# Low halves of w_out in the last forgetting head: two GpSimd operations instead of one on VectorE

## The chip, the cores and the metric

One core of a Trainium2 chip runs the whole layer. The time is device microseconds (us) of one execution, and the figure compared is the median of several executions. Engines are named as in the profile: PE (TensorE, matmuls), PEld (its weight loads), DVE (VectorE), ACT (ScalarE), POOL (GpSimd), SP (SyncE, which here only issues DMAs).

## The reference, cut to what matters

One decoder layer, 2048 tokens, width 1024. Two mixers share one normalised and modulated input and one input projection: 8 heads of forgetting attention (causal softmax with a cumulative log-gate bias) and 8 heads of sliding-window attention. Both are gated, put side by side and sent through w_out (1024 x 1024).

```python
oa = forgetting_attention(qa, ka, va, fa + b_fgate[l])
oa = oa * jax.nn.silu(za)
...
ob = ob * jax.nn.silu(zb)
y = jnp.concatenate([oa, ob], axis=-1) @ w_out[l]
x = x + gate[:, None, :] * rms_norm(y, g_post[l])
```

## The kernel before, in words

All large products are done in float16 with each operand split into a high and a low half, so that high x high, high x low and low x high add up to nearly float32. A split is always the same pair of steps: ScalarE writes the high half (a scaled copy, rounded to float16), then another engine subtracts it from the scaled value and writes the rest as the low half.

The order of the work is written out by hand. Each engine runs its instructions in program order; an instruction that waits holds up those behind it on its engine. The forgetting heads run as 160 steps, 20 for each head (`Step`). In the loop over the steps, `s` is the step, `hd` the head and `r` the step within the head. A step does in turn:

- ScalarE exponentials of the scores (`exp32`, L1263), 128 x up to 1024 float32 into a tile called p;
- the subtraction of the step before on VectorE (`low`, L1270), p minus its high half, both in SBUF; this is the operation called pha in the profile;
- in the last head (`hd == 7`) the split of one or two tiles of w_out (`w_out_split`, L1345 and L1346);
- half of the step's fillers, the high half of p on ScalarE (L1267), the score matmuls of the next step (L1256 to L1259, the tile sta), the value matmuls of two steps before (L1280 to L1283), and the rest of the fillers.

Fillers are, until the middle of the last head, matmuls for row maxima of the scores (L1207), which VectorE reduces from PSUM (L1210, L1212); from step 10 of the last head on they are units of the output product (`Out.product`, L1405, three matmuls each: high x high, oz high x w low, oz low x w high). Before its product an output block is turned: PE transposes it (L1368), VectorE multiplies by the gate path (L1377, in place in T), ScalarE squares it (L1381, tile zj), VectorE and ScalarE split it (tile oz, L1391 and L1392).

w_out is cut into 16 tiles m of 128 x 512 float32 (m modulo 8 is the row block k, m // 8 the column half). A table gives the step of the last head in which each is split:

```python
w_at = {2: [0], 3: [1], 4: [2], 5: [3], 6: [4], 8: [5], 10: [6], 11: [7], 12: [8], 13: [9], 14: [10],
        15: [11, 12], 16: [13, 14], 17: [15]}
```

Loads (L1340, on SP) are issued three steps ahead into a ring of 6 buffers (`stp`), which also takes the junk outputs zj (L1381) and yj (L1414) of ScalarE. A buffer is given out again when all its readers are done. Both halves go into one resident tile, wohl; the product reads row block k of the first column half from unit 0 on (step 10) and of the second half from unit 16 on (step 15). So tiles 11 to 15, split in steps 15 to 17, are read by PE in steps 16 and 17.

GpSimd runs the product of the rotary embedding (L711, early in the program), small copies, and issues DMAs. Its last instruction before the end is the DMA of a z tile at 969.20 us, ahead of the first split.

Of the kernel before, what the change touches and what calls it, by code (L numbers as in the profile page):

```python
# [15 lines left out]
ALU = mybir.AluOpType  # L16
# [24 lines left out]
def hybrid_layer(  # L41
# [17 lines left out]
    V, A, G, PE, SP = nc.vector, nc.scalar, nc.gpsimd, nc.tensor, nc.sync  # L59
# [97 lines left out]
    wsc = const.tile([P, KT], F32, name="wsc")  # L157
# [1156 lines left out]
    def w_slot(n):  # L1314
        return oio["w"][:, n // KT, n % KT, :]
# [26 lines left out]
    def w_out_split(m):  # L1342
        k, cc = m % KT, slice((m // KT) * CH, (m // KT + 1) * CH)
        raw, hi = w_raw.pop(m), w_slot(k)[:, cc]
        A.activation(hi, raw[:], AF.Copy, scale=wsc[:, k:k + 1])  # L1345
        V.scalar_tensor_tensor(w_slot(8 + k)[:, cc], raw[:], wsc[:, k:k + 1], hi, op0=ALU.mult, op1=ALU.subtract)  # L1346

    oio = {}

# [117 lines left out]
    with tc.manual_schedule():  # L1467
# [27 lines left out]
        for s, stp_ in enumerate(steps):  # L1495
# [28 lines left out]
            if hd == 7:  # L1524
                for m in w_at.get(r, []):
                    w_out_split(m)
# [70 lines left out]
```

## Time and profile before

| | |
|---|---|
| time, median of 3 executions | 1220.45 us (1219.6 to 1221.59) |
| span of the profiled execution | 1218.0 us |
| its own time | not recorded beside the span |
| PE busy | 1164.0 us, 96% |
| VectorE busy | 907.5 us, 75% |
| ScalarE busy | 675.5 us, 55% |
| GpSimd busy | 142.1 us, 12% |
| the 16 w_out subtractions on VectorE (L1346) | 984.8 to 1037.2 us, 745 ns median |
| the 16 high halves on ScalarE (L1345) | 982.3 to 1036.4 us, 709 ns median |

Busy time says how long an engine had work; a busy share is an average over stages with different limits, so the change has to be read in its own stretch. Rows of the timeline read: start, duration, engine, line, operation, output <- inputs, and in brackets how long the engine sat idle before it and what ended that. Rows of one line's instructions give minimum/median/maximum in ns, then the first and last start. Rows of the windows give the stretch, its length, and the busy us (with the count) of PE, PEld, DVE, ACT and POOL, then the granted PE clock (1.00 is full), the DMA share and GB/s.

### The profile page before, as it was taken

What the parts mean: (1) busy time and instruction counts of PE and PEld (TensorE: products, weight loads), DVE (VectorE), ACT (ScalarE), POOL (GpSimd) and SP (SyncE); (2) the same over time, 40 slices, a digit from 0 to 9 for tenths busy, and PEclk for the clock granted to TensorE, in tenths of its full rate; (3) what the DMA queues carried; (4) which work ended last, traced back from release to release, by engine and by line L of the source; (5) the groups of instructions that cost most, each with busy time, mean ns of one, the idle gap of its engine ahead of it and who ended that gap; (6) DMA issues with size and microseconds to landing.
All of it is one profiled execution on the core that took longest, in us unless ns stands there. A gap on an engine that the chain in (4) does not pass through costs nothing.

```text
span 1218.0 us, 27395 instructions
## 1 busy us (share of the span) xinstructions
PE 1164.0 (96%) x10832; PEld 695.9 (57%) x10832; DVE 907.5 (75%) x2268; ACT 675.5 (55%) x1117; POOL 142.1 (12%) x252
## 2 busy tenths in 40 slices
PE   6789999999999999999999999999999979999996
PEld 2457545865558976555555555555555545555553
DVE  6766557676776747688888798878978797666665
ACT  2666445555655452566667666666766778333231
POOL 2011133223232211011010110010000000000000
PEclk9899999999999999999999999999999989999999
DMA  9554332323323322323334323122111135445652
GB/s 325 187 146 139 81 89 79 86 56 103 93 69 86 57 58 52 76 59 84 83 60 84 86 61 79 39 71 49 38 46 42 58 118 186 144 156 190 202 167 81
DMA packets 88036, 120.71 MB, mean 99 GB/s; under 512 B 27836, under 2 KB 63716, under 8 KB 87908
## 3 DMA queue, kind: packets, MB, share of 16 engines
q1 hardware_dynamic: 76932, 85.94, 23.5%
q0 software_dynamic: 10976, 33.03, 11.6%
q8 instruction: 85, 1.39, 0.6%
q14 instruction: 43, 0.35, 0.1%
HBM read 71.56 MB, written 25.18 MB: 79 GB/s over the span
## 4 chain that ended last, share of the span: by engine, by line
PE 77%; DVE 9%; DMA 5%; issue 3%; ACT 2%; SPq 2%; POOL 1%; DVEq 0%; ACTq 0%; POOLq 0%
PE bk L307 29%; PE bk L1405 12%; PE bk L325 7%; PE sta L1256 4%; PE bk L1207 4%; PE sta L1257 4%; PE poa L1282 2%; PE poa L1283 2%; PE poa L1280 2%; PE pxb L864 2%; PE pss L831 2%; PE pob L883 2%; DVE pha L1270 1%; DVE a_m L1210 1%; PE bk L1368 1%
## 5 line engine op out<-in xcount | busy, mean ns | idle before, releaser
L1263 ACT ACTIVATE p<-sta,lift,scl_qk 128x1024 f32<-128x1024 f32 (+2 forms) x160 | 172.0, 1075 | 135.3 <-PE sta L1257 76.8
L307 PE MATMUL bk<-hT,wh_qk 128*128 128x512 f16 x768 | 194.6, 378 | 0.4 <-DVE a_m L1210 0.4
L1405 PE MATMUL bk<-wohl,oz 128*128 128x512 f16 x768 | 172.4, 379 | 1.7 <-ACT wohl L1345 0.8
L1210 DVE TENSOR_REDUCE a_m<-bk 128x1 f32<-128x512 f32 x192 | 130.2, 685 | 52.4 <-PE bk L1207 51.7
L1270 DVE TENSOR_TENSOR pha<-p,pha 128x1024 f16<-128x1024 f32 (+2 forms) x160 | 169.0, 1056 | 0.0
L1267 ACT ACTIVATE pha<-p 128x1024 f16<-128x1024 f32 (+2 forms) x160 | 148.0, 925 | 5.9 <-PE poa L1283 0.9
L1405 PEld LDWEIGHTS <-oz 128*128 128x128 f16 x768 | 74.4, 99 | 83.7 <-issue 1.8
L1280 PE MATMUL poa<-vt,pha 128*128 128x65 f16 x1088 | 117.4, 193 | 2.7 <-DVE ona L1289 2.7
L1283 PE MATMUL poa<-vt,pha 128*128 128x65 f16 x1088 | 117.2, 193 | 1.1 <-DVE pha L1270 1.1
L1282 PE MATMUL poa<-vt,pha 128*128 128x64 f16 x1088 | 117.5, 195 | 0.0
L1256 PE MATMUL sta<-T 128*128 128x512 f16 (+1 forms) x320 | 112.2, 351 | 4.7 <-ACT p L1263 4.6
L307 PEld LDWEIGHTS <-wh_qk 128*128 128x128 f16 x768 | 72.4, 97 | 75.2 <-issue 1.4
L1280 PEld LDWEIGHTS <-pha 128*128 128x128 f16 x1088 | 102.4, 97 | 17.4 <-DVE ona L1289 3.8
L1207 PE MATMUL bk<-T 66*128 66x512 f16 (+2 forms) x320 | 109.9, 350 | 2.0 <-DMA T<-stq 1.5
L1257 PE MATMUL sta<-T 69*128 69x512 f16 (+1 forms) x320 | 111.1, 352 | 0.0
L1282 PEld LDWEIGHTS <-pha 128*128 128x128 f16 x1088 | 101.5, 97 | 11.5 <-issue 0.3
L1283 PEld LDWEIGHTS <-pha 128*128 128x128 f16 x1088 | 101.5, 99 | 1.3 <-DVE pha L1270 1.3
L307 PE MATMUL bk<-hT,wh_za 128*128 128x512 f16 x384 | 99.8, 378 | 0.0
L325 PE MATMUL bk<-wh_va,hT 128*128 128x128 f16 x1536 | 91.0, 219 | 0.6 <-issue 0.6
L307 PE MATMUL bk<-hT,wh_zb 128*128 128x512 f16 x384 | 89.9, 379 | 1.1 <-DVE wh_zb L251 1.1
L325 PEld LDWEIGHTS <-hT 128*128 128x128 f16 x1536 | 87.4, 98 | 5.7 <-issue 3.1
L307 PE MATMUL bk<-hT,wh_qb 128*128 128x512 f16 x384 | 87.2, 379 | 0.0
(491 smaller groups left out, 1886.1 us busy)
## 6 DMA issues: line engine op xcount, KB each, us to landing
wa<-in_w_ada_dram SPq DMA_DIRECT2D x16, 512.0 KB
z_d<-tz POOLq DMA_DIRECT2D x32, 256.0 KB, 3.5
T<-stq SPq DMA_DIRECT2D x128, 64.0 KB
T<-o_d SPq DMA_DIRECT2D x16, 512.0 KB
T<-z_d SPq DMA_DIRECT2D x16, 512.0 KB
xr<-in_x_dram SPq DMA_DIRECT2D x16, 512.0 KB
out_dram<-yg SPq DMA_DIRECT2D x15, 512.0 KB
xt<-in_x_dram SPq DMA_DIRECT2D x12, 512.0 KB
```

The source lines that it names most:

```text
L307: PE.matmul(ps, whl[:, a, k, :], hT[ci][:, b, k, :], start=(k == 0 and n == 0), stop=(k == KT - 1 and n == 2))
L325: PE.matmul(ps[:, u * P:(u + 1) * P], hT[ci][:, a, k, u * P:(u + 1) * P], whl[:, b, k, :], start=(k == 0 and n == 0), stop=(k == KT - 1 an ...
L1207: PE.matmul(mx[:, :w], T[0:XM, 0, i * P:(i + 1) * P], T[0:XM, 2, pc * CH:pc * CH + w], start=True, stop=True)
L1256: PE.matmul(self.st[:, o:o + w], T[:, 3, kb_], T[:, 1, qc], start=True, stop=False)
L1257: PE.matmul(self.st[:, o:o + w], T[0:XR, 2, kb_], T[0:XR, 0, qc], start=False, stop=not diag)
L1263: A.activation(self.p32[:, :self.w], self.st[:, :self.w], AF.Exp, scale=scl[f"qk{self.hd}"][:], bias=lift[:])
L1267: A.activation(self.ph[:, 0, :self.w], self.p32[:, :self.w], AF.Copy)
L1270: V.tensor_tensor(self.ph[:, 1, :self.w], self.p32[:, :self.w], self.ph[:, 0, :self.w], op=ALU.subtract)
L1280: PE.matmul(po[:, u, :], ph[:, 0, pq], vt[:, b, hd, 0:65], start=(self.first and n == 0 and u == 0), stop=False)
L1282: PE.matmul(po[:, u, 0:64], ph[:, 0, pq], vt[:, b, hd, 65:VW], start=False, stop=False)
L1283: PE.matmul(po[:, u, :], ph[:, 1, pq], vt[:, b, hd, 0:65], start=False, stop=(self.last and n == len(self.blocks) - 1))
L1405: PE.matmul(py, self.hl[:, i, k, :], w_slot(8 * j + k)[:, cc], start=(k == 0 and m_ == 0), stop=(k == KT - 1 and m_ == 2))
```

## The change

`w_out_split` no longer subtracts on VectorE. GpSimd first scales the raw tile in place, then subtracts the high half from it:

```diff
         A.activation(hi, raw[:], AF.Copy, scale=wsc[:, k:k + 1])
-        V.scalar_tensor_tensor(w_slot(8 + k)[:, cc], raw[:], wsc[:, k:k + 1], hi, op0=ALU.mult, op1=ALU.subtract)
+        G.tensor_scalar(raw[:], raw[:], wsc[:, k:k + 1], None, op0=ALU.mult)
+        G.tensor_tensor(w_slot(8 + k)[:, cc], raw[:], hi, op=ALU.subtract)
```

Since the scaling writes the tile that ScalarE reads, it has to wait for ScalarE's high half; the subtraction waits for the scaling. Lines below L1346 move down by one (L1377 becomes L1378, L1405 becomes L1406).

On VectorE, at the first two tiles (steps 2 and 3 of the last head), the subtractions go and nothing else moves. The wo names are raw tiles of w_out, wohl the resident halves, pha and p the halves and the exponentials of a step, bk PSUM banks:

```order
 L1210 TENSOR_REDUCE a_m<-bk_134 128x1
 L1270 TENSOR_TENSOR pha<-p_14278,pha 128x384
-L1346 SCALAR_TENSOR_TENSOR wohl<-wo_14272,wsc,wohl 128x512
 L1212 ISA bk_135,a_m<-bk_135,cmask 128x128
 L1212 ISA a_m 128x1
```

Each stood right behind a pha subtraction, and the reductions behind it move up by one place.

On GpSimd, behind its last DMAs and at the end of the program, there now stand 32 instructions, two for each tile; these are the first of them, after the z tiles:

```order
 L349 DMA z_d<-tz 128x512 x6
-L1593 UNCONDITIONAL_BRANCH
-L1593 ISA
+L1346 TENSOR_SCALAR wo_14272<-wo_14272,wsc 128x512
+L1347 TENSOR_TENSOR wohl<-wo_14272,wohl 128x512
+L1346 TENSOR_SCALAR wo_14274<-wo_14274,wsc 128x512
+L1347 TENSOR_TENSOR wohl<-wo_14274,wohl 128x512
```

and these the last, tiles 11 to 15, which PE reads at once:

```order
+L1346 TENSOR_SCALAR wo_14776<-wo_14776,wsc 128x512
+L1347 TENSOR_TENSOR wohl<-wo_14776,wohl 128x512
+L1346 TENSOR_SCALAR wo_14778<-wo_14778,wsc 128x512
+L1347 TENSOR_TENSOR wohl<-wo_14778,wohl 128x512
+L1346 TENSOR_SCALAR wo_14830<-wo_14830,wsc 128x512
+L1347 TENSOR_TENSOR wohl<-wo_14830,wohl 128x512
+L1346 TENSOR_SCALAR wo_14832<-wo_14832,wsc 128x512
+L1347 TENSOR_TENSOR wohl<-wo_14832,wohl 128x512
+L1346 TENSOR_SCALAR wo_14873<-wo_14873,wsc 128x512
+L1347 TENSOR_TENSOR wohl<-wo_14873,wohl 128x512
```

All tiles now pass through one engine in turn, two operations each, with no other work of that engine between them. Loads, junk outputs and product units that waited for VectorE's subtraction of a tile wait for GpSimd's; the order of PE, ScalarE and SP is the same.

## The prediction

> **What bounds the kernel now.** I read the busy shares first, then the 2 and 10 us windows around the last forgetting head, then single instructions there in order of time.
>
> ```profile
> span 1218.0 us, 27395 instructions
> PE 1164.0 (96%) x10832; PEld 695.9 (57%) x10832; DVE 907.5 (75%) x2268; ACT 675.5 (55%) x1117; POOL 142.1 (12%) x252
> 980.00:990.00 10.00, 6.49 (x70) 3.54 (x70) 9.83 (x23) 9.12 (x12) 0.00 (x0) 1.00 0.22 67
> 990.00:1000.00 10.00, 9.21 (x105) 6.00 (x106) 10.00 (x18) 6.26 (x8) 0.00 (x0) 0.83 0.74 236
> 1020.00:1030.00 10.00, 10.00 (x83) 5.15 (x81) 5.53 (x8) 8.15 (x12) 0.00 (x0) 1.00 0.59 191
> 1030.00:1040.00 10.00, 8.79 (x106) 5.52 (x103) 7.90 (x11) 8.94 (x13) 0.00 (x0) 1.00 0.01 2
> ```
>
> Over the span PE is the bound (96%). The change touches only the stretch from 982 to 1038 us. In the window rows (length, then busy us of PE, PEld, DVE, ACT and POOL, then the granted PE clock) it has three parts: until 1000 VectorE has no idle time (9.83 and 10.00 of 10 us) and PE waits (6.49); at 1020 to 1030 PE is full and VectorE half idle (5.53); at 1030 to 1040 PE waits again. GpSimd is empty throughout.
>
> **What is removed.** Sixteen VectorE operations:
>
> ```profile
> L1346 DVE SCALAR_TENSOR_TENSOR wohl<-wo,wsc,wohl x16: 743/745/752, 984.8 to 1037.2; 128x512 f16<-128x512 f32 x16
> 986.84 1.21 DVE L1270 TENSOR_TENSOR pha<-p,pha 128x1024 f16<-128x1024 f32 x1
> 987.97 0.74 DVE L1346 SCALAR_TENSOR_TENSOR wohl<-wo,wsc,wohl 128x512 f16<-128x512 f32 x1
> 988.63 0.68 DVE L1210 TENSOR_REDUCE a_m<-bk 128x1 f32<-128x512 f32 x1
> ```
>
> Durations overlap a little; from start to start one costs 988.63 - 987.97 = 0.66 us, and a 1024-wide pha subtraction 1.13. Five (m = 0 to 4) stand in the stretch where VectorE is the bound: 5 x 0.66 = **3.3 us** off the path. The other eleven lie where VectorE has idle time or the product waits for them.
>
> **What is added.** Each tile gets two GpSimd operations in place of one on VectorE. The subtraction has a direct neighbour, the same shape with two inputs; the scaling has none:
>
> ```profile
> L711 POOL TENSOR_TENSOR qs<-qs,sinT x20: 1256/1269/1356, 63.7 to 385.2; 128x512 f32<-128x512 f32 x20
> L499 POOL TENSOR_SCALAR_AFFINE_SELECT bm<-zero 128x256 f32<-128x256 f32 x1 | 0.4, 414 | 0.0
> L842 POOL COPY sm__1821<-snk 128x2 f32<-128x2 f32 x2 | 0.3, 194 | 0.0
> ```
>
> Subtraction: 1.27 us. Scaling, unknown: the one-input rows give (414 - 194) / 254 = 0.87 ns per element, so 194 + 510 x 0.87, about 0.65 us; its ends are 0.41 (half the width) and 1.27 (the two-input operation). I take 0.65, the one-input slope, and 0.04 for each of two handovers (a guess): a pair is **2.0 us**. The Trainium skill (GPSIMD Engine Reference, section 3.1) gives 769 ns for a 512-element loop; with that a pair would be 2.1 and the sum 1.2 us higher; no row here shows it.
>
> **Who blocks whom.** Does work on GpSimd leave VectorE alone? Rows where the rotary product (L711) overlapped VectorE:
>
> ```profile
> 63.70 1.27 POOL L711 TENSOR_TENSOR qs<-qs,sinT 128x512 f32<-128x512 f32 x1 [55.63 <-DMA qs<-qf]
> 64.71 1.47 DVE L251 SCALAR_TENSOR_TENSOR wh_zb<-wr_zb,w_sw,wh_zb 128x512 f16<-128x512 f32 x2 [0.41 <-ACT wh_zb L245]
> L251 DVE SCALAR_TENSOR_TENSOR wh_zb<-wr_zb,w_sw,wh_zb x8: 740/745/808, 64.7 to 312.4; 128x512 f16<-128x512 f32 x8
> L384 DVE TENSOR_SCALAR xt<-xt,rst x8: 748/748/1755, 85.3 to 112.5; 128x1024 f32<-128x1024 f32 x8
> L848 DVE TENSOR_SCALAR b_nb<-b_m x32: 169/170/694, 161.1 to 425.4; 128x4 f32<-128x4 f32 x32
> ```
>
> It does not. A VectorE scaling went from 0.75 to 1.76 us, a tiny one from 0.17 to 0.69. The kind that matters, two inputs in SBUF, met GpSimd once, in the last 0.26 us of its operation, and took 808 instead of 745 ns: 0.06 lost of 0.26 possible. The pha subtraction (L1270) has two SBUF inputs, one for each step of the head. I take a wait to the end of the GpSimd operation; the ends are none and a full 1.27 for each. The skill (SBUF — State Buffer, Who interferes with whom) says of this kind that it contends with a GpSimd instruction that reads SBUF and that the loser blocks fully; by it the sum is my forecast, by 0.06 us a wait the first stretch would gain 3.0 instead. The 63 ns agree in sign only.
>
> **First stretch, worked out.** GpSimd may start on a tile when ScalarE's high half is done (L1345):
>
> ```profile
> 982.28 0.72 ACT L1345 ACTIVATE wohl<-wo,wsc 128x512 f16<-128x512 f32 x1
> 984.94 0.71 ACT L1345 ACTIVATE wohl<-wo,wsc 128x512 f16<-128x512 f32 x1
> 987.48 0.71 ACT L1345 ACTIVATE wohl<-wo,wsc 128x512 f16<-128x512 f32 x1
> 982.15 1.08 DVE L1270 TENSOR_TENSOR pha<-p,pha 128x896 f16<-128x896 f32 x1
> 984.30 0.55 DVE L1270 TENSOR_TENSOR pha<-p,pha 128x384 f16<-128x384 f32 x1
> 990.12 1.22 DVE L1270 TENSOR_TENSOR pha<-p,pha 128x1024 f16<-128x1024 f32 x1
> 993.12 1.08 DVE L1270 TENSOR_TENSOR pha<-p,pha 128x896 f16<-128x896 f32 x1
> 995.86 0.55 DVE L1270 TENSOR_TENSOR pha<-p,pha 128x384 f16<-128x384 f32 x1
> 998.19 1.27 DVE L1377 TENSOR_TENSOR T<-bk,T 128x512 f32<-128x512 f32 x2
> ```
>
> Tile 0: scaling after the pha operation in progress, 983.20 to 983.85; subtraction to 985.17. VectorE's next pha, ready at 984.30, waits 0.87. Tile 1: scaling 985.70, subtraction 986.40 to 987.67; the pha of 986.84, now 0.21 late, waits 0.62. Tile 2: after that pha, subtraction to 990.82; the next waits 0.53. Likewise 0.82 and 0.92 for the pha operations of 993.12 and 995.86, since GpSimd is behind by then and busy without a break. Waits of 0.87 + 0.62 + 0.53 + 0.82 + 0.92 = 3.76 against 3.30 saved: **+0.5 us** at L1377 (998.19), on which ScalarE's squares and the next scores hang. Ends: -3.3 (no wait) and 5 x 1.27 - 3.3 = +3.1.
>
> **Middle (m = 5 to 10): 0.** What hides a late low half is PE's own work (10.00 of 10 us) and one to eight steps between split and use (closest: tiles 7 and 10, one step). Behind waiting instructions stand: on SP the later w_out loads, which wait for a buffer that GpSimd now frees, and behind them an o_d store and the loads of x; on ScalarE the junk outputs (zj, yj), which take the same buffers, and behind them the next exponentials. None comes due before a pair has finished; if the cover is gone, each costs up to one pair, 2.0.
>
> **Last tiles.** Tiles 11 to 15 come in a burst, and PE uses them at once:
>
> ```profile
> 1028.39 1.32 ACT L1345 ACTIVATE wohl<-wo,wsc 128x512 f16<-128x512 f32 x2
> 1031.65 1.32 ACT L1345 ACTIVATE wohl<-wo,wsc 128x512 f16<-128x512 f32 x2
> 1029.13 1.21 DVE L1270 TENSOR_TENSOR pha<-p,pha 128x1024 f16<-128x1024 f32 x1
> 1031.59 1.22 DVE L1270 TENSOR_TENSOR pha<-p,pha 128x1024 f16<-128x1024 f32 x1
> 1035.25 1.22 DVE L1270 TENSOR_TENSOR pha<-p,pha 128x1024 f16<-128x1024 f32 x1
> 1037.16 0.75 DVE L1346 SCALAR_TENSOR_TENSOR wohl<-wo,wsc,wohl 128x512 f16<-128x512 f32 x1 [0.70 <-ACT wohl L1345]
> 1034.28 2.10 PE L1405 MATMUL bk<-wohl,oz 128*128 128x512 f16 x9
> 1037.97 0.59 PE L1405 MATMUL bk<-wohl,oz 128*128 128x512 f16 x2 [0.41 <-DVE wohl L1346]
> ```
>
> Today the last low half is ready at 1037.91 and PE, which waited 0.41 for it, goes on. GpSimd can begin tile 11 at 1029.1 and needs five pairs, 10.0 us, plus the three pha subtractions that take turns with it, 3 x 1.13 = 3.4: ready at 1042.5, so **+4.6 us**. PE has nothing else then: L1405 stands in front of the next scores. After 1040 the end of the program is a PE chain, so the delay is passed on whole. Ends: without turns 1029.1 + 10.0 = 1039.1, +1.2; with the scaling at 1.27 (pairs of 2.6) and four turns, 1029.1 + 13.1 + 4.5 = 1046.7, +8.8.
>
> **Sum.** +0.5 + 0 + 4.6 = +5.1 us: the span goes from 1218.0 to 1223.1. The profiled execution's own time is not among the records; its span is 2.45 below the median of 1220.45, so the time is 1220.45 + 5.1 = **1225.5 us**.
>
> **Rivals.**
>
> *VectorE wins the turns.* If a waiting VectorE operation, or one issued in the same moment, always goes first, the first stretch keeps its 3.3 and only the tail pays: -3.3 + 4.6 = +1.3, 1221.8. For it: all three long cases above can also be read as GpSimd merely having started first. Against: in all five cases worked out above GpSimd is already in its subtraction when the pha operation becomes ready.
>
> *The clock falls in the tail.* After two stretches of PE waiting the granted clock (last but two) halved:
>
> ```profile
> 988.00:990.00 2.00, 0.32 (x8) 0.15 (x6) 1.97 (x6) 2.00 (x4) 0.00 (x0) 1.00 0.00 0
> 992.00:994.00 2.00, 2.00 (x27) 1.52 (x26) 2.00 (x4) 1.12 (x2) 0.00 (x0) 0.50 0.46 135
> 1000.00:1002.00 2.00, 0.21 (x1) 0.10 (x1) 1.97 (x5) 2.00 (x4) 0.00 (x0) 0.88 0.67 203
> 1002.00:1004.00 2.00, 2.00 (x12) 1.18 (x11) 1.86 (x7) 1.60 (x3) 0.00 (x0) 0.50 0.01 4
> 1000.00:1010.00 10.00, 8.12 (x71) 5.66 (x70) 8.41 (x18) 8.69 (x12) 0.00 (x0) 0.66 0.52 165
> ```
>
> From 1034 to 1042 PE would run three groups of 0.65 us and wait otherwise, as thin as 988 to 990. The first fall took 10 x (1 - 0.83) = 1.7 us of PE's work, the second 10 x (1 - 0.66) = 3.4: 1227.2, up to 1228.9.
>
> *Faster: GpSimd does not hold VectorE.* The first stretch gives 3.3, and with the squares 3.3 earlier PE's idle time before 1001.8 goes, so that the half clock after 1002 (at least 1.7 of PE's work) is not granted; the tail costs its lower end, 1.2: -3.3 - 1.7 + 1.2 = -3.8, 1216.6; with the clock as it is -2.1, 1218.3. It decides where the five waits together stay below 3.3 - 1.2 = 2.1 us, 0.42 each. For it: the one overlapping two-input operation lost 63 ns. Against: it met only the end of a GpSimd operation.
>
> *Slow scaling.* With 1.27 for it: +3.1 at most and +8.8, 1232.
>
> **How the numbers follow.** Forecast 0.42; clock 0.22; VectorE wins 0.14; not held 0.15 (half of it with the clock gained); slow scaling 0.07. The range reaches from 1217.5 (part of the not-held case) to 1231: left out are 0.07 below, and 0.07 with a part of the clock case above. About 0.2% (2.4 us) is what a measurement tells from no change, so faster means below 1218.0 and slower above 1222.9. Faster 0.13 (not held, most of it, and the spread of the others), same 0.20 (VectorE wins, the rest of not held, the forecast's low edge), slower 0.67.
>
> **What would show it.** Scaling near 0.65 and subtraction near 1.27 us on GpSimd; pha subtractions (L1270) between 982 and 998 of 1.8 to 2.1 us instead of 1.2; L1378 (L1377 before) of the first block within 1 us of 998.2; PE waiting 4 to 5 us for GpSimd's L1347 between 1032 and 1043; and the granted clock after 1040. Unchanged pha durations would make the prediction wrong in its first term and most of its last; a tail wait under 2 us, in its size.

## The result and the profile after

The changed kernel takes 1229.24 us (median of 4, 1228.83 to 1230.65) against 1220.87 (median of 4, 1219.6 to 1221.59): ratio 1.0067, 95% interval 1.0051 to 1.0082, which is +8.2 us (6.2 to 10.0). Slower, as forecast, and inside the range, but 8.2 where the sum said 5.1. The profiled execution took 1230.65 with a span of 1228.9, the longest of the four.

The two added operations and the engine that waits for them, in the rows of one line (minimum/median/maximum ns, first and last start) and of PE's waits (us in total, times, longest):

```profile
L1346 POOL TENSOR_SCALAR wo<-wo,wsc x16: 1559/1569/2917, 986.1 to 1043.5; 128x512 f32<-128x512 f32 x16
L1347 POOL TENSOR_TENSOR wohl<-wo,wohl x16: 1150/1157/1551, 987.8 to 1045.2; 128x512 f16<-128x512 f32 x16
PE bk L1406 <- POOL wohl L1347: 7.7, 6, 2.0
```

The scaling takes 1.57 us, not the 0.65 of the sum, and is longer than the two-input subtraction behind it (1.16). Unhindered, a pair is 2.78 us from start to start (1040.74 to 1043.52 below). The first stretch, VectorE and then GpSimd:

```profile
985.20 1.08 DVE L1270 TENSOR_TENSOR pha<-p,pha 128x896 f16<-128x896 f32 x1
989.22 1.49 DVE L1270 TENSOR_TENSOR pha<-p,pha 128x1024 f16<-128x1024 f32 x1
992.12 1.38 DVE L1270 TENSOR_TENSOR pha<-p,pha 128x1024 f16<-128x1024 f32 x1
994.61 1.53 DVE L1270 TENSOR_TENSOR pha<-p,pha 128x896 f16<-128x896 f32 x1
997.14 0.60 DVE L1270 TENSOR_TENSOR pha<-p,pha 128x384 f16<-128x384 f32 x1
999.29 1.29 DVE L1378 TENSOR_TENSOR T<-bk,T 128x512 f32<-128x512 f32 x2 [0.36 <-DMA T<-z_d]
```

```profile
988.95 1.56 POOL L1346 TENSOR_SCALAR wo<-wo,wsc 128x512 f32<-128x512 f32 x1
991.72 1.57 POOL L1346 TENSOR_SCALAR wo<-wo,wsc 128x512 f32<-128x512 f32 x1
994.51 1.57 POOL L1346 TENSOR_SCALAR wo<-wo,wsc 128x512 f32<-128x512 f32 x1
```

To compare these rows with those of before: the pha row of 985.20 stands ahead of the first split and was at 982.15, so this execution was 3.05 us late before any changed instruction. Other executions below are 0.2 to 5.6 late at that row, with the same program up to it. All positions are therefore counted from this row (the **anchor**). The T row (L1378) then comes 14.09 behind it, against 998.19 - 982.15 = 16.04: the first stretch **gained** 1.95 us, where I had a loss of 0.5. The last four of the five pha operations lost 0.28 + 0.16 + 0.45 + 0.05 = 0.94 against their rows of before, not 3.76, and the first (987.35, not shown) lost nothing. With the 3.30 saved and the 0.36 us that the T row waited for its load of z_d, this accounts for the stretch: 3.30 - 0.94 - 0.36 = 2.00.

In the middle, one wait that was not in the sum:

```profile
1014.33 1.87 DVE L1393 SCALAR_TENSOR_TENSOR oz<-T,w_pw,oz 128x1024 f16<-128x1024 f32 x1 [0.22 <-ACT oz L1392]
1015.11 2.92 POOL L1346 TENSOR_SCALAR wo<-wo,wsc 128x512 f32<-128x512 f32 x1
1019.32 0.59 PE L1406 MATMUL bk<-wohl,oz 128*128 128x512 f16 x2 [0.78 <-POOL wohl L1347]
```

Here GpSimd is the one that is held up: its scaling of tile 7 reaches 2.92 us beside VectorE's split of oz and the pha operation behind that (0.55 us at 1016.13, not shown), the pair ends late, and PE stands 0.78 us. In the tail, GpSimd's rows and PE's:

```profile
1030.98 2.58 POOL L1346 TENSOR_SCALAR wo<-wo,wsc 128x512 f32<-128x512 f32 x1 [1.43 <-ACT wohl L1345]
1036.43 1.55 POOL L1347 TENSOR_TENSOR wohl<-wo,wohl 128x512 f16<-128x512 f32 x1
1040.74 1.56 POOL L1346 TENSOR_SCALAR wo<-wo,wsc 128x512 f32<-128x512 f32 x1
1043.52 1.56 POOL L1346 TENSOR_SCALAR wo<-wo,wsc 128x512 f32<-128x512 f32 x1
1045.17 1.15 POOL L1347 TENSOR_TENSOR wohl<-wo,wohl 128x512 f16<-128x512 f32 x1
```

```profile
1034.86 0.59 PE L1406 MATMUL bk<-wohl,oz 128*128 128x512 f16 x2 [0.86 <-POOL wohl L1347]
1038.03 0.81 PE L1406 MATMUL bk<-wohl,oz 128*128 128x512 f16 x3 [0.77 <-POOL wohl L1347]
1040.81 0.81 PE L1406 MATMUL bk<-wohl,oz 128*128 128x512 f16 x3 [1.97 <-POOL wohl L1347]
1043.59 1.44 PE L1406 MATMUL bk<-wohl,oz 128*128 128x512 f16 x3 [1.97 <-POOL wohl L1347]
1046.37 1.01 PE L1406 MATMUL bk<-wohl,oz 128*128 128x512 f16 x2 [1.34 <-POOL wohl L1347]
```

PE waits 6.91 us in the tail. GpSimd runs five pairs without a gap from 1030.98 to 1045.17 + 1.15 = 1046.32. Three such matmuls take 0.81 us at 1040.81 and 1.44 at 1043.59: the clock has fallen between. By windows of 2 us the granted clock is 1.00 at 1038 to 1040, 0.98 at 1040 to 1042 and 0.50 at 1042 to 1044. The windows of 10 us show the same, first before, then after the change (PE busy first, granted clock third from the end):

```profile
1040.00:1050.00 10.00, 8.90 (x118) 5.68 (x115) 7.46 (x24) 4.45 (x7) 0.00 (x0) 1.00 0.00 1
```

```profile
1040.00:1050.00 10.00, 5.87 (x35) 2.85 (x35) 0.69 (x1) 1.71 (x4) 6.15 (x5) 0.60 0.01 2
```

From the last low half to the end of the span it is 1228.9 - 1046.32 = 182.58 us, against 1218.0 - 1037.91 = 180.09: another 2.5. So, in positions from the anchor: -1.95 to the T row, +0.69 to the pha operation of 1030.92 (1029.13 before), +6.62 to the last low half, +2.49 behind it: 7.85 in all.

### The profile page after: what moved, and what is told of

The parts are those of the page before. It is cut to its first block, busy times and chain, and to the rows that moved or that the text cites. A ratio compares the mean times of both kernels' runs of the same rounds, so it can differ in the third digit from the quotient of the medians.

```text
span 1228.9 us, 27422 instructions
## 1 busy us (share of the span) xinstructions
PE 1167.3 (95%) x10832; PEld 696.9 (57%) x10832; DVE 900.8 (73%) x2252; ACT 675.2 (55%) x1117; POOL 190.2 (15%) x284
## 5 line engine op out<-in xcount | busy, mean ns | idle before, releaser
L1406 PE MATMUL bk<-wohl,oz 128*128 128x512 f16 x768 | 175.0, 382 | 8.8 <-POOL wohl L1347 7.7
L1406 PEld LDWEIGHTS <-oz 128*128 128x128 f16 x768 | 74.7, 100 | 92.2 <-issue 10.7
```

The source lines that it names most:

```text
L1406: PE.matmul(py, self.hl[:, i, k, :], w_slot(8 * j + k)[:, cc], start=(k == 0 and m_ == 0), stop=(k == KT - 1 and m_ == 2))
```

## The experiments

The theory after the result: **the burst**. Tiles 11 to 15 pass through GpSimd at 2.8 us each while PE reads them at once; the waits and the half clock make up the loss, and the early tiles are a small gain. Rivals: GpSimd costs VectorE time wherever they meet (**holding**); the late start of the profiled execution belongs to the changed program (**offset**). Each ratio is to the kernel before, with its 95% interval.

### Tiles 11 to 15 back on VectorE, and the mirror image

```diff
+        if m < 11:
             G.tensor_scalar(raw[:], raw[:], wsc[:, k:k + 1], None, op0=ALU.mult)
             G.tensor_tensor(w_slot(8 + k)[:, cc], raw[:], hi, op=ALU.subtract)
+        else:
+            V.scalar_tensor_tensor(w_slot(8 + k)[:, cc], raw[:], wsc[:, k:k + 1], hi, op0=ALU.mult, op1=ALU.subtract)
```

> Tiles 0 to 10 split by GpSimd as in the changed kernel, tiles 11 to 15 by VectorE as before. Theory A (burst): the whole loss comes from tiles 11 to 15, whose GpSimd pairs of 2.8 us PE waits for, and the half clock after them; the first stretch gained about 2 us. Then the PE waits for L1347 go from 7.7 to under 0.5 us, the granted clock at 1040 to 1050 is 1.00 again, and the time is 1220.9 - 2.0 = 1218.9 (1217.5 to 1220). Theory B (holding): GpSimd takes time from VectorE wherever the two meet, in the middle tiles too; then eleven of sixteen tiles keep their share and the time stays at 1222 or above. Theory C (offset): the 3.05 us that the profile of the changed kernel was late before its first changed instruction belongs to the changed program; then 1222 at the least.

The mirror image has `if m >= 11` in place of `if m < 11`.

> The mirror image: tiles 0 to 10 on VectorE as before, tiles 11 to 15 on GpSimd. Theory A: the tail loses its 7.3 us of waiting and 2.5 us behind the last subtraction, and no gain of the first stretch stands against it: 1220.9 + 9.8 = 1230.7, about 2 us slower than the changed kernel (1229.5 to 1232). Theory B: only five of sixteen tiles pay, and the time is about 1220.9 + 8.4 x 5/16 = 1223.5. PE waits for L1347 near 8 us by A, near 3 by B.

Measured: 0.9992 (0.9981 to 1.0003) with the tail on VectorE, 1.0086 (1.0069 to 1.0103) with only the tail on GpSimd, +10.5 us (8.4 to 12.6). This speaks for the burst and against the offset: five tiles cost no less than all sixteen (1.0067), and the profile of the first kernel is only 0.85 us late at its anchor. The mirror image:

```profile
983.88 1.08 DVE L1270 TENSOR_TENSOR pha<-p,pha 128x896 f16<-128x896 f32 x1
1045.11 1.15 POOL L1348 TENSOR_TENSOR wohl<-wo,wohl 128x512 f16<-128x512 f32 x1
```

Ahead of its tail all stands as before the change (the T row 16.04 behind the anchor, the pha operation at the tail's start 46.99), and the last low half comes 62.38 behind it, against 55.76. So the tail alone costs 6.6 us, what it cost in the changed kernel, and the rest of the program 1.95 more (1228.3 - 1046.26 = 182.04), 8.6 in all by the trace. PE's waits for GpSimd are 6.1 us, not the 8 expected.

The first kernel kept half of what was expected:

```profile
983.00 1.08 DVE L1270 TENSOR_TENSOR pha<-p,pha 128x896 f16<-128x896 f32 x1
997.07 1.29 DVE L1381 TENSOR_TENSOR T<-bk,T 128x512 f32<-128x512 f32 x2
1017.42 0.59 PE L1409 MATMUL bk<-wohl,oz 128*128 128x512 f16 x2 [0.77 <-POOL wohl L1348]
1029.01 1.22 DVE L1270 TENSOR_TENSOR pha<-p,pha 128x1024 f16<-128x1024 f32 x1
```

It leads by 1.97 us at the T row (14.07 behind the anchor, against 16.04) and by 0.97 at the last row (46.01, against 46.98); between them stands the wait for tile 7, so my "under 0.5 us" of PE waits for GpSimd failed.

### Only tiles 0 to 4 on GpSimd

```diff
-        if m < 11:
+        if m < 5:
```

> Only tiles 0 to 4 on GpSimd, tiles 5 to 15 on VectorE as before. The kernel with tiles 0 to 10 on GpSimd was 1.97 us ahead at the first T row and 0.97 ahead at 1029; between them PE waited 0.77 us for tile 7's GpSimd subtraction. Theory M (that wait is what was given back): without it the first stretch's gain stays, 1220.9 - 1.9 = 1219.0, ratio 0.998, no PE wait for GpSimd, and the pha operation at about 1029 comes 1.5 to 2 us earlier than before, after allowing for the stretch ahead of the first split. Rival (the gain is lost in any case, to the next wait for ScalarE or to the half clock): 1220 to 1221.

Measured: 0.9983 (0.9971 to 0.9995).

```profile
1032.22 1.22 DVE L1270 TENSOR_TENSOR pha<-p,pha 128x1024 f16<-128x1024 f32 x1
```

In its trace PE waits for GpSimd nowhere, and this pha operation leads by 2.55 us (1032.22 - 987.79 = 44.43, against 46.98), where 1.5 to 2 were expected. The lead at the T row (1.92) is kept, as theory M has it; by the times alone this kernel and the one with eleven tiles are not told apart, since their intervals overlap.

### All tiles on GpSimd, one a step

```diff
-        w_at = {2: [0], 3: [1], 4: [2], 5: [3], 6: [4], 8: [5], 10: [6], 11: [7], 12: [8], 13: [9], 14: [10],
-                15: [11, 12], 16: [13, 14], 17: [15]}
+        w_at = {2: [0], 3: [1], 4: [2], 5: [3], 6: [4], 7: [5], 8: [6], 9: [7], 10: [8], 11: [9], 12: [10],
+                13: [11], 14: [12], 15: [13, 14], 16: [15]}
```

> All tiles on GpSimd as in the changed kernel, but split about one a step from step 7 on (5 in step 7, 6 in 8, 7 in 9, 8 in 10, 9 in 11, 10 in 12, 11 in 13, 12 in 14, 13 and 14 in 15, 15 in 16), so that no tile is read within a pair's time. Theory A (burst): GpSimd has the throughput (a pair of 2.8 to 4.2 us against steps of 3 to 4), PE waits for its subtractions fall from 8.5 us to under 1, the clock at 1040 to 1050 is 1.00, and the time is 1219 to 1221. Rival (what GpSimd takes from VectorE costs anyway, wherever it stands): 1224 or above.

Measured: 1.0008 (0.9997 to 1.0019), so 7.2 us of the 8.2 are gone with every GpSimd operation still there. The granted clock at 1040 to 1050 is 1.00. The holding rival (1224 or above) falls: on the scale of 1220.87 this is 1221.9 (1220.5 to 1223.2). It is also a little above the 1219 to 1221 that theory A gave.

```profile
1038.08 0.59 PE L1406 MATMUL bk<-wohl,oz 128*128 128x512 f16 x2 [1.97 <-POOL wohl L1347]
```

This is PE's one wait for GpSimd, for tile 15, still the third pair of a small burst, and not the "under 1" that I expected.

### Is it the scale, the form, or the operation?

```diff
-        G.tensor_scalar(raw[:], raw[:], wsc[:, k:k + 1], None, op0=ALU.mult)
+        G.tensor_tensor(raw[:], raw[:], wsc[:, k:k + 1].broadcast_to([P, CH]), op=ALU.mult)
```

> The changed kernel with the scaling written as a two-input product with the scale broadcast along the row. Expected 1.16 us for it, as for the subtraction, instead of 1.57: a pair of 2.37 instead of 2.78, so 5 x 0.41 = 2.0 us less in the tail (PE waits 5.7 instead of 7.7). Theory H (each kind holds VectorE's two-input operations for a part of its own: the trace reads as 0.56 us of the scaling's 1.57 and 1.02 of the subtraction's 1.16): the two-input scaling holds VectorE 0.46 us longer, the pha subtractions of the first stretch lose 2 to 4 us together instead of 0.94, and the time is 1227 to 1229. Rival (the part held is the same whatever the form): they lose about 0.9 still, and the time is 1226 to 1227.

```diff
-        G.tensor_scalar(raw[:], raw[:], wsc[:, k:k + 1], None, op0=ALU.mult)
+        G.tensor_scalar(raw[:], raw[:], 1.0, None, op0=ALU.mult)
```

> The changed kernel with the scaling by the constant 1.0 in place of the per-partition scale (so the low halves are not those of the scaled weights). If the scale read from a tile is what makes the scaling 1.57 us instead of the 0.65 of my sum, it falls to 0.6 to 0.8, a pair to about 1.9, and the tail by 5 x 0.9 = 4.5 us and the clock: 1222 to 1225. If the operation itself has that price, 1.57 stays and the time is that of the changed kernel, 1228 to 1230.

Measured: 1.0069 (1.0045 to 1.0092) and 1.0064 (1.0044 to 1.0083). The scaling's rows, of the broadcast product and of the constant:

```profile
L1346 POOL TENSOR_TENSOR wo<-wo,wsc x16: 1030/1040/2066, 987.3 to 1046.0; 128x512 f32<-128x512 f32 x16
```

```profile
L1346 POOL TENSOR_SCALAR wo<-wo x16: 1479/1491/2517, 985.0 to 1042.0; 128x512 f32<-128x512 f32 x16
```

The scale read from a tile is worth 0.08 us; the scalar operation itself is the dear one, and the two-input product is cheaper by half a microsecond. Yet the kernel with the cheaper scaling is no faster: on the scale of 1220.87 it takes 1229.3, and theory H had 1227 to 1229. Its first stretch loses what theory H said, for the most part through another cause:

```profile
986.32 1.08 DVE L1270 TENSOR_TENSOR pha<-p,pha 128x896 f16<-128x896 f32 x1
988.47 1.48 DVE L1270 TENSOR_TENSOR pha<-p,pha 128x384 f16<-128x384 f32 x1
991.29 1.96 DVE L1270 TENSOR_TENSOR pha<-p,pha 128x1024 f16<-128x1024 f32 x1
994.65 1.81 DVE L1270 TENSOR_TENSOR pha<-p,pha 128x1024 f16<-128x1024 f32 x1
997.59 1.96 DVE L1270 TENSOR_TENSOR pha<-p,pha 128x896 f16<-128x896 f32 x1
1000.54 0.97 DVE L1270 TENSOR_TENSOR pha<-p,pha 128x384 f16<-128x384 f32 x1
1002.62 1.27 DVE L1378 TENSOR_TENSOR T<-bk,T 128x512 f32<-128x512 f32 x2
```

```profile
988.39 1.15 POOL L1347 TENSOR_TENSOR wohl<-wo,wohl 128x512 f16<-128x512 f32 x1
994.22 1.16 POOL L1347 TENSOR_TENSOR wohl<-wo,wohl 128x512 f16<-128x512 f32 x1
1000.05 1.04 POOL L1346 TENSOR_TENSOR wo<-wo,wsc 128x512 f32<-128x512 f32 x1 [1.46 <-ACT wohl L1345]
```

The first pha operation behind a subtraction, 0.08 us after its start, takes 1.48 instead of 0.55: held until 988.47 + 0.93 = 989.40, 1.01 us into the subtraction's 1.15. In the changed kernel the pha operations behind a scaling were held until 0.55, 0.56 and 0.55 us into its 1.57 (989.50 - 988.95, 992.28 - 991.72, 995.06 - 994.51). With two-input operations only, the five pha operations lost 0.93 + 0.75 + 0.59 + 0.88 + 0.42 = 3.57 us, and the T row is 0.26 later than before (1002.62 - 986.32 = 16.30).

Only the last of the five stands behind the product (1000.05), which held it for 0.91 of its 1.04. The four before it stand behind the subtraction, which is the same in the changed kernel; it held them until 1.01 to 1.03 us into it. So the product does hold longer than the scalar form, as theory H has it, but most of the loss comes from where the pha operations fall: with the shorter pair they become ready during the subtraction. The kernel with a half scaling below keeps the scalar form, and its pha operations lose 2.96 us, all but 0.12 of it behind the subtraction. What the cheaper scaling gave back in the tail (+5.2 us there against +6.6) the first stretch took.

### The clock: PE kept busy while it waits

```diff
+            if (self.t, n) == (0, 1):
+                for _ in range((0, 0, 0, 3, 3, 8, 8, 5)[k]):
+                    PE.matmul(py, self.hl[:, 0, k - 1, :], w_slot(k - 1)[:, cc], start=False, stop=False)
             for m_, (i, j) in enumerate(((0, 0), (0, 1), (1, 0))):
```

> The changed kernel with 27 matmuls more in front of the five units that wait for tiles 11 to 15 (3, 3, 8, 8, 5), repeating a high product of the unit before, so that PE works while it waits; their sums are added to that block, so the output differs. Theory K (the half clock at 1040 to 1050 comes from PE standing idle): the granted clock there goes from 0.60 to 0.95 or more, the end of the program comes 2.5 us sooner after the last subtraction (180.1 us as before the change, not 182.6), and the time is 1226 to 1227. Rival (the clock follows something else, or its loss is hidden): the clock stays below 0.8 and the time is 1228.5 to 1231, the added matmuls costing up to 1 us.

Measured: 1.0037 (1.0024 to 1.0049), 3.7 us less than the changed kernel with 27 matmuls more.

```profile
1040.00:1050.00 10.00, 8.62 (x64) 4.32 (x62) 1.38 (x4) 2.94 (x6) 6.06 (x5) 1.00 0.01 2
1041.15 1.89 PE L1407 MATMUL bk<-wohl,oz 128*128 128x512 f16 x8
1043.50 0.59 PE L1409 MATMUL bk<-wohl,oz 128*128 128x512 f16 x2 [0.24 <-POOL wohl L1347]
1045.07 1.15 POOL L1347 TENSOR_TENSOR wohl<-wo,wohl 128x512 f16<-128x512 f32 x1
```

The clock stays at 1.00, and from the last low half to the end of its span (1226.1) it is 179.88 us, as before the change. GpSimd's last operation is no earlier than in the changed kernel (61.65 behind the anchor of 984.57, against 61.12), so the gain is the clock's alone: 2.7 us by the trace (182.58 - 179.88), 3.7 by the times (0.0030 of 1220.87; with the two intervals put together 1.2 to 6.1). The time is 1225.4 on that scale, a little under the 1226 to 1227 of theory K.

### A pair of the size that the prediction used

```diff
-        G.tensor_scalar(raw[:], raw[:], wsc[:, k:k + 1], None, op0=ALU.mult)
+        G.tensor_scalar(raw[:, 0:CH // 2], raw[:, 0:CH // 2], wsc[:, k:k + 1], None, op0=ALU.mult)
```

> The changed kernel with the GpSimd scaling on the left 256 of 512 columns only (the low halves of the right ones are then wrong), which should take about 0.8 us and make a pair 2.0, the size that the prediction worked with. Theory S (the size of the scaling is what the prediction missed in the tail): five pairs are 5 x 0.75 = 3.8 us shorter, PE waits for L1347 fall from 7.7 to about 4, and the time is 1222.5 to 1225.5, where the prediction stood. Rival (the wait is set by turns with VectorE and ScalarE's high halves, not by the pair): the waits stay above 6 and the time above 1227.

Measured: 1.0056 (1.0043 to 1.0069), +6.8 us: neither of the two.

```profile
984.17 1.08 DVE L1270 TENSOR_TENSOR pha<-p,pha 128x896 f16<-128x896 f32 x1
1000.89 1.28 DVE L1378 TENSOR_TENSOR T<-bk,T 128x512 f32<-128x512 f32 x2
1031.55 1.22 DVE L1270 TENSOR_TENSOR pha<-p,pha 128x1024 f16<-128x1024 f32 x1
```

```profile
1040.58 0.92 POOL L1346 TENSOR_SCALAR wo<-wo,wsc 128x256 f32<-128x256 f32 x1
1042.71 0.92 POOL L1346 TENSOR_SCALAR wo<-wo,wsc 128x256 f32<-128x256 f32 x1
1043.72 1.15 POOL L1347 TENSOR_TENSOR wohl<-wo,wohl 128x512 f16<-128x512 f32 x1
```

With a pair of 2.13 us PE waits 5.0 us for GpSimd, not 4, and the terms of the prediction come out near what was worked out:

- first stretch +0.68 (16.72 against 16.04), where I had +0.5. The agreement is in part luck: the pha operations lost 2.96, not 3.76, and VectorE waited another 0.84 for row maxima from PE, whose granted clock was 0.50 at 992 to 998;
- the pha operation at the tail's start +0.40 (47.38), and the last low half +4.94 (60.70 against 55.76), so +4.5 for the tail, where I had +4.6. Here too two errors meet: the five pairs are 0.65 us longer than the 10.0 of the sum, and the turns with VectorE 0.85 shorter than its 3.4 (2.55);
- behind it 1227.1 - 1044.87 = 182.23, +2.1 for the clock, which the sum had left to a rival.

What my expectation here forgot is the first stretch: a shorter scaling loses the 1.95 us that the long one gained.

### A version that beats both

The tiles of the tail split sooner, on top of tiles 0 to 4 on GpSimd:

```diff
+        w_at = {2: [0], 3: [1], 4: [2], 5: [3], 6: [4], 8: [5], 9: [6], 10: [7], 11: [8], 12: [9, 10],
+                13: [11], 14: [12], 15: [13, 14], 16: [15]}
```

> Tiles 0 to 4 on GpSimd, the others on VectorE, and the tiles of the tail split about a step sooner (6 in step 9, 7 in 10, 8 in 11, 9 and 10 in 12, 11 in 13, 12 in 14, 13 and 14 in 15, 15 in 16). If PE's waits at 1034 to 1038 in the kernel before (0.98 for ScalarE's high half, 0.41 for VectorE's low half) come from the burst alone, they go: 1 to 1.4 us less than with tiles 0 to 4 alone, 1217.5 to 1218. If ScalarE and VectorE are full there in any case, the waits move to another place and the time is that of tiles 0 to 4 alone, within 0.5 us.

The same table with all tiles on VectorE:

> The kernel before, all tiles on VectorE, with the table of the kernel that measured 0.9975 (6 in step 9, 7 in 10, 8 in 11, 9 and 10 in 12, 11 in 13, 12 in 14, 13 and 14 in 15, 15 in 16). If the two edits add up, the table alone gives what the pair has over tiles 0 to 4 alone, 0.9975 against 0.9983, so 0.999 to 0.9995, 1219.5 to 1220.9, and GpSimd's part stays worth about 2 us. If the table does it all, this kernel reaches 1218 as well.

Measured: 0.9975 (0.9965 to 0.9985), -3.1 us, for both edits, and 0.9988 (0.9979 to 0.9997) for the table alone. With 0.9983 for tiles 0 to 4 alone the two add up within their intervals; by the same intervals the kernel with both edits is not told apart from tiles 0 to 4 alone. In both traces with this table PE waits for no w_out half any more, only for oz; in that of both edits:

```profile
L1409 PE MATMUL bk<-wohl,oz 128*128 128x512 f16 x768 | 172.1, 379 | 1.7 <-DVE oz L1396 1.7
```

## Why the prediction was right in sign and short in size

**Scaling (0.65, ends 0.41 and 1.27): wrong, the step that failed.** It is 1.57 us, above the upper end. The slope came from a 256-wide select and a 2-wide copy; this operation takes 0.92 for 256 columns and 1.57 for 512, so 2.5 ns per element where I had 0.87, and the price of the two-input operation was no upper bound. The subtraction (1.27 taken, 1.16 measured) was a little high. The rival with a slow scaling (0.07) is the one whose condition came, and more than that; its two terms (+3.1 at most and +8.8) were both too high.

**Who blocks whom: right in kind, wrong in length.** A pha operation behind a GpSimd operation is held, but not always to its end: 1.01 us of the subtraction's 1.15, only 0.55 of the scaling's 1.57. The one row that the prediction had shows the same when it is read by position: the operation of 64.71 lost 0.06, so it was held until 64.77, 1.07 us into the 1.27 of the product of 63.70. It goes the other way too: GpSimd's scaling took 2.92 us beside VectorE's oz and pha operations. The Trainium skill (SBUF — State Buffer, Who interferes with whom) calls the pair of ports that the two engines share an exclusive lock; that whoever issues first keeps it for the whole instruction and blocks the other fully, it says of VectorE's two-port modes, and the prediction carried this over to two inputs in SBUF. By that the pha operation of 994.61 would have waited 1.5 us for the scaling, and the trace shows 0.45; for the subtraction it comes near, with 0.93 us lost of 1.07.

The rival in which VectorE wins every turn falls as a rule: the pha operations of 994.61 here and of 988.47 with the two-input scaling waited. What it foretold, that the first stretch keeps its gain and only the tail pays, is close to what came, for another reason.

**First stretch (+0.5): wrong sign, -1.95.** Its working had GpSimd in its subtraction each time a pha operation became ready. With a scaling of 1.57 it is in the scaling instead, past or near its short hold, and the subtractions fall beside VectorE's reductions from PSUM. The gain is the phase that the long scaling happens to set: with the half scaling the same stretch is +0.68, with the two-input scaling +0.26.

**Middle (0): 0.7 short.** "None comes due before a pair has finished" failed for tile 7, one of the two that I had named as closest: the pair took 2.92 + 1.16 us behind VectorE's oz, and PE waited 0.78.

**Tail (+4.6): mechanism right, +6.6.** Five pairs of 2.78 are 13.9 instead of 10.0; turns with VectorE cost 1.4 (15.34 from 1030.98 to 1046.32, less 13.9) instead of 3.4. With a pair of 2.13 the tail measured +4.5. That pair replaces the scaling's row in the sum, which is why I call the scaling's size the main fault; the turns were counted too dear, and that hid a part of it.

**The clock: set aside as a rival at 0.22, and it happened.** Between 1038.84 and 1043.59 PE ran three matmuls (0.81 us) and the granted clock halved; +2.5 in the trace, inside the 1.7 to 3.4 that the rival gave, and keeping PE busy took that off again. It should have been a term: the waits that my own sum gave PE in the tail were as thin as the stretches that it quoted. The forecast of +5.1 and the clock's 2.1 make 7.2, and the kernel with a pair of 2.13 measured 6.8.

**The error that cancelled.** Against the kernel with the half scaling, the whole one cost 2.1 us more in the tail (6.62 against 4.54) and 1.0 in the middle (+0.69 against -0.28), and returned 2.6 in the first stretch (-1.95 against +0.68). So the time hardly shows it: 1.0067 and 1.0056, intervals that overlap. The forecast fell short by about the clock, although its most wrong number was the scaling; that is read only from positions in the trace.

## What to carry to other kernels

Before work goes to a slower engine, look for the place where its results are read at once: there, as in this tail, its whole duration counts, times the tiles of the burst, and an average load of 15% says nothing. Move only the pieces whose readers are far off, and split the burst by starting it sooner. And where a sum gives TensorE a row of waits, the clock belongs in the sum.

## What the runs showed of the hardware that was not expected

- GpSimd multiplies 128 x 512 float32 by one scale per partition in 1.57 us as a scalar operation, by a constant in 1.49, and as a two-input product with the scale broadcast in 1.04.
- Its operations hold VectorE's two-input operations for different parts of themselves: 0.55 of 1.57 us for the scalar form (three rows), 1.01 to 1.03 of 1.15 for the subtraction (eight rows in the kernels with the two-input and the half scaling), 0.91 of 1.04 for the two-input product (one row). These are lengths read from overlaps in the traces; why they differ was not tried.
- PE's granted clock halved within 4.75 us that had 0.81 of work in them (1038.84 to 1043.59). Two shorter waits stood ahead of them (0.86 and 0.77), and their part was not tried; with nearly the same waits the kernel with only the tail on GpSimd lost its clock sooner (0.66 at 1040 to 1042, against 0.98). One wait of 1.97 us alone, with the tiles one a step, left it at 1.00. And 27 matmuls of no use kept it at full speed and made the kernel faster, 1.0037 against 1.0067.
